# A two-layer hybrid encoder block on one core: start-up order, spread rope groups, a later transpose of the retention's output, and one early up chunk

## The chip, the core and the metric

The kernel runs on one core of a Trainium2 chip. Its engines work side by side, each from its own queue in its own order: TensorE (PE; the load of its stationary operand is listed as PEld), VectorE (DVE), ScalarE (ACT), GpSimd (POOL) and SyncE (SP, which issues most DMAs). An instruction waits for semaphores that other engines or DMAs raise, and everything behind it on its own queue waits with it. The metric is the device time in microseconds of one execution, in the median of the runs shown.

## What is computed

The reference runs two layers over a stream h of 512 tokens by 1024 channels in float32. Cut to what matters here:

```
u = rms_norm(h, norm_mix_pre[i])
proj = u @ w_in[i]
qa, ka, va, qr, kr, vr, gr, gate_a, gate_b = jnp.split(proj, splits, axis=-1)
att = dilated_attention_mixer(qa, ka, va)
ret = retention_mixer(qr, kr, vr, gr, ret_decay_logit[i])
merged = (jax.nn.sigmoid(gate_a) * (att @ w_att_out[i])
          + jax.nn.sigmoid(gate_b) * (ret @ w_ret_out[i]))
h = h + rms_norm(merged @ w_out[i], norm_mix_post[i])
u = rms_norm(h, norm_mlp_pre[i])
ff = jnp.square(jax.nn.relu(u @ w_mlp_up[i])) @ w_mlp_down[i]
h = h + rms_norm(ff, norm_mlp_post[i])
gate = jax.nn.sigmoid(rms_norm(h) @ w_ple_gate[i])
h = h + gate * rms_norm(p[i] @ w_ple_proj[i], norm_ple[i])
```

Attention has 8 heads of 64 channels, with rotary on 16 of them. Retention has 8 heads with keys of 64 and values of 128 channels, rotary on all key channels, two directions with a decay each, and each head's output is normalised over its 128 channels (group norm) before it is gated by silu(g).

## The kernel before

**Precision and weights.** Every float32 factor of a large product is split into a high part (an ACT copy to fp32r) and a low part (a subtraction, on DVE or POOL); each product is three matmuls, high by high, high by low and low by high (the table HL). The weights are packed on the host into chunks of 128 x 1024, in the order of the table PLAN. `prefetch` (L273) loads chunks on SP into tiles raw, copies the high part on ACT (L278) and subtracts the low part in `low` (L301); five split chunks (wt) are alive at a time, and `chunk` keeps about four ahead of their use. The low part of the kinds in POOL_LOW goes to POOL in two of three chunks, in two halves of 512 columns, and so do the chunks of POOL_MORE; all others go to DVE.

**Tokens.** The 512 tokens stand in four tiles of 128. `pre_norm` (L393) takes the sum of squares of a tile's two halves on ACT, adds 1e-6 to the first sum on DVE (L353), adds the two and takes the power -0.5 on POOL (`rstd_of`, L359 and L361), and scales on DVE (L403 or L406). Its inner function `rest` is put in a list: eight transposes on PE (L413), and the split into uT, high on ACT (L416), low on DVE (L417). `step` is called after each main step of PE, some six matmuls of 512 columns, and runs the oldest entry of the list when it is old enough. START gives these ages for tokens 1 to 3 at the start of the first layer.

**Order on PE.** PE's order is that of the program text (manual schedule); the other engines' order is made by the scheduler, by priority and readiness. The main jobs of a layer run in the order va, the attention's rope groups (q and k, twice), then rope q and k of the retention, vr, g 0 to 3, rope q and k, vr, and the a and g jobs. Beside them runs a generator `sides` (the attention's heads, then the retention's), which `tick` advances by 0.94 pieces for each main step from the end of the attention's rope groups on. A rope group is two chunks (8 main steps), and ends with some eight DVE and two ACT instructions of 512 columns.

**A retention head** (L583 to L633) is seven pieces: four score tiles (two matmuls each, L590 and L591, then a DVE product with the decay and a split into rt), `finish` of the head before (transposes of y, L576, and the gate), the product with v (12 matmuls, L612) with its ACT copy yt (L615), and the transposes of yt (L620) with the statistics (L624 to L627), the root on POOL (L628) and the scaling into y on DVE (L630). So between a head's L620 and its L576 stand the four score tiles of the next head. Behind the last head two empty pieces stand ahead of `finish`. `decay` makes the next head's decay table.

**Decays.** `decays` (L425) makes the logarithms of the decays from 32 numbers, in 25 small DVE instructions and one on ACT. It is called behind the va job of the first layer; its input tile dk comes by a DMA that is issued in it (L429).

**The up projection.** Behind w_out come eight products of the PLE projection (pp, evacuated in turn by ACT and DVE, L794 and L796), and then the first EARLY = 3 up chunks in two token halves (L871), 256 columns each: all chunks for tokens 0 and 1, and then all for tokens 2 and 3. The other up chunks run over all 512 tokens at once.

**The start.** L980 to L1005: token 0's rows in two halves, chunks 0 to 3, tokens 1 to 3, with `pre_norm` of token 0, its `rest` at once (flush), and the first splits between them.

Of the kernel before, what the change touches and what calls it, by code (L numbers as in the profile page):

```python
# [9 lines left out]
F32 = mybir.dt.float32  # L10
F32R = mybir.dt.float32r
# [18 lines left out]
POOL_MORE = [("pp",0),("pp",1)]  # L30
# [18 lines left out]
START = (2, 5, 7)  # L49
AGE_PP = 8  # L50
EARLY = 3
# [11 lines left out]
def _slot(e):  # L63
# [136 lines left out]
def block(ctx: ExitStack, tc: tile.TileContext, x, pT, w, dl, gains, cs, lc, rel, eye, out):  # L200
# [192 lines left out]
    def pre_norm(h, t, gain, upd=None):  # L393
        un = blk("P", [P, D], name="un")
        sq = []
        for n, sl in enumerate(HALVES):
            if upd:
                upd(sl)
            sq.append(sumsq(h[:, sl], un[:, sl], None if n else 1e-6))
        r = rstd_of(*sq)  # L400
        for sl in HALVES:
            if gain is None:
                nc.vector.tensor_scalar(un[:, sl], h[:, sl], r, None, op0=ALU.mult)  # L403
            else:
                g = gain[sl.start // S] if isinstance(gain, list) else gain[:, sl]
                nc.vector.scalar_tensor_tensor(un[:, sl], h[:, sl], r, g, op0=ALU.mult, op1=ALU.mult)  # L406

        def rest():
            unready.discard(t)
            for q in range(2):  # L410
                ps = bank("tp")
                for k in range(4):
                    nc.tensor.transpose(ps[:, k * P:(k + 1) * P], un[:, (4 * q + k) * P:(4 * q + k + 1) * P], ident)  # L413
                p3 = ps.rearrange("p (k n) -> p k n", k=4)
                hi = uT[:, 0, 4 * q:4 * q + 4, t * P:(t + 1) * P]
                nc.scalar.activation(hi, p3, AF.Copy)  # L416
                nc.vector.tensor_tensor(uT[:, 1, 4 * q:4 * q + 4, t * P:(t + 1) * P], p3, hi.bitcast(F32), op=ALU.subtract)  # L417

        unready.add(t)
        pending.append((clock[0], rest))  # L420
# [138 lines left out]
    def ret_heads(i, relt, gT, retT):  # L559
# [22 lines left out]

        for h in range(8):  # L583
# [4 lines left out]
            for k in range(NT):  # L588
# [11 lines left out]
                yield 1  # L600
            if late:
                finish(*late)
# [3 lines left out]
            y = t2("y")  # L606
            y3 = y.rearrange("p (t e) -> p t e", t=NT)
# [7 lines left out]
            nc.scalar.activation(yt, o, AF.Copy)  # L615
            yield 1
            o = bank("tp")
            o3 = o.rearrange("p (t e) -> p t e", t=NT)
            for t in range(NT):
                nc.tensor.transpose(o3[:, t, :], yt[:, t * P:(t + 1) * P], ident)  # L620
            mv = sm.tile([P, NT, 2], F32, name="mv", tag="mv", bufs=3)
            for t in range(NT):
                st = sm.tile([P, 6], F32, name="st", tag="st", bufs=4)
                nc.vector.bn_stats(st, o3[:, t, :])  # L624
                nc.vector.bn_aggr(mv[:, t, :], st)
            ve, rs = col(NT, name="ve"), col(NT, name="rs")
            nc.vector.tensor_scalar(ve, mv[:, :, 1], 1e-5, 16.0, op0=ALU.add, op1=ALU.mult)  # L627
            nc.gpsimd.tensor_tensor(rs, ve, half, op=ALU.pow)  # L628
            for t in range(NT):
                nc.vector.tensor_scalar(y3[:, t, :], o3[:, t, :], mv[:, t, 0:1], rs[:, t:t + 1],  # L630
                                        op0=ALU.subtract, op1=ALU.mult)
            yield 1
            late = (h, y3)  # L633
# [5 lines left out]
    def one_layer(i, h):  # L639
# [12 lines left out]
        if i == 0:  # L652
            decays()
# [107 lines left out]
        def evac_wo(hf):  # L761
            @soon
            def f(t, ps):
                hs_ = HALVES[hf]
                ssq[t][hf] = sumsq(ps, t2("junk"), None if hf else 1e-6)
# [20 lines left out]
        for hf in range(2):  # L786
            hsl = slice(hf * S, (hf + 1) * S)
            ch = chunk(i, "pp", hf)
            for t in range(NT):
                ps = bank(PP_BANKS[4 * hf + t])  # L790
                for k in range(2):
                    row_mm(ps, ch, k, lambda a, k, t: phl[k][:, a, t * P:(t + 1) * P], k, t, k == 0, k == 1)
                if t % 2:
                    nc.scalar.activation(pn[t][:, hsl], ps, AF.Copy)  # L794
                else:
                    nc.vector.tensor_copy(pn[t][:, hsl], ps)  # L796
                step(AGE_PP)
# [131 lines left out]
        def evac_dn(hf):  # L929
            @soon  # L930
            def f(t, ps):
                a = acc[t][hf]
                nc.vector.tensor_tensor(a, ps, a, op=ALU.subtract if hf else ALU.add)
                ssq[t][hf] = sumsq(a, t2("junk"), None if hf else 1e-6)
# [51 lines left out]
    nc.vector.memset(ones[:, :P], 1.0)  # L986
    prefetch(2, 0)
    nc.sync.dma_start(h[1], x[P:2 * P, :])
    prefetch(4, 0)
    for t in (2, 3):  # L990
# [46 lines left out]
```

## Time and profile before

| | us |
|---|---|
| median of 3 runs | 1794.63 (1794.54 to 1794.65) |
| the profiled execution | 1794.64 |
| its span, first to last instruction | 1792.9 |
| PE busy | 1772.4 (8209 matmuls) |
| DVE busy | 1145.4 |
| ACT busy | 807.5 |
| POOL busy | 382.6 |

Times in the profile are microseconds from the span's start, those marked ns excepted. L12 is line 12 of the kernel. A group's row has the line, the engine, the operation, its result and operands by the program's names, and how often it ran. The ends of matmuls are modelled, since they are pipelined: the distance from one matmul's start to the next tells more than the duration shown.

### The profile page before, as it was taken

How to read it: one execution, taken by the hardware profiler on the slowest of the kernel's cores; microseconds unless marked ns; L12 is line 12 of the kernel's file. 1: busy time of each engine (PE TensorE's matmuls, PEld its weight loads, DVE VectorE, ACT ScalarE, POOL GpSimd, SP SyncE). 2: the span in 40 equal slices, each digit the busy share in tenths (PEclk: the TensorE clock that was granted, in tenths of full speed). 3: DMA queues.
4: the chain of work that ended last, by engine and by line, in shares of the span. 5: the costliest groups of instructions: out<-in, count | busy, mean ns of one | idle time of the engine just before them, and what ended most of it. 6: DMA issues, size and time to landing. Idle time of an engine off the chain costs nothing.

```text
span 1792.9 us, 22127 instructions
## 1 busy us (share of the span) xinstructions
PE 1772.4 (99%) x8209; PEld 1466.2 (82%) x8209; DVE 1145.4 (64%) x1803; ACT 807.5 (45%) x1271; POOL 382.6 (21%) x354
## 2 busy tenths in 40 slices
PE   8999999999999999999999999999999999999998
PEld 6888788888898888888788887888888888888887
DVE  6676777743465677674656767677444657667754
ACT  4255444332466454433443555444333664444342
POOL 2312244311142001002123222442012410000030
PEclk9999999999999999999999999999999999999999
DMA  5555464552347655552346545555422566664421
GB/s 213 194 193 159 149 212 137 166 175 95 117 142 188 165 158 161 156 184 70 129 141 214 165 145 172 184 159 187 136 101 99 165 170 156 169 175 130 165 71 60
DMA packets 87807, 274.58 MB, mean 153 GB/s; under 512 B 11921, under 2 KB 20497, under 8 KB 87698
## 3 DMA queue, kind: packets, MB, share of 16 engines
q1 hardware_dynamic: 80786, 247.99, 40.7%
q0 software_dynamic: 6912, 25.17, 8.3%
q8 instruction: 65, 1.06, 0.2%
q14 instruction: 44, 0.36, 0.1%
HBM read 239.55 MB, written 33.55 MB: 152 GB/s over the span
## 4 chain that ended last, share of the span: by engine, by line
PE 89%; DVE 4%; POOL 2%; ACT 2%; issue 1%; DMA 1%; SPq 0%; POOLq 0%; ACTq 0%
PE acc L312 28%; PE acc L322 19%; PE s L312 18%; PE acc L849 8%; PE tp L849 4%; PE tp L612 2%; PE tp L544 2%; PE tp L507 2%; PE acc L871 1%; PE tp L413 1%; POOL wt L301 1%; PE s L525 1%; PE s L526 1%; PE s L590 1%; PE s L871 1%
## 5 line engine op out<-in xcount | busy, mean ns | idle before, releaser
L312 PE MATMUL acc<-uT,wt 128*128 128x512 f32 x1920 | 472.8, 392 | 0.0
L312 PEld LDWEIGHTS acc<-uT,wt 128*128 128x128 f32 x1920 | 356.2, 188 | 71.8
L301 DVE TENSOR_TENSOR wt<-raw,wt 128x1024 fp32r<-128x1024 f32 x217 | 279.4, 1292 | 187.6 <-ACT wt L278 187.1
L278 ACT ACTIVATE wt<-raw 128x1024 fp32r<-128x1024 f32 x280 | 293.9, 1055 | 223.0 <-PE acc L312 114.0
L322 PE MATMUL acc<-wt,uT 128*128 128x512 f32 x1320 | 320.8, 396 | 4.4 <-ACT uT L416 1.8
L312 PE MATMUL s<-uT,wt 128*128 128x512 f32 x1392 | 323.7, 389 | 0.0
L312 PEld LDWEIGHTS s<-uT,wt 128*128 128x128 f32 x1392 | 261.1, 188 | 54.1
L322 PEld LDWEIGHTS acc<-wt,uT 128*128 128x128 f32 x1320 | 245.6, 189 | 55.6 <-DVE uT L417 2.6
L301 POOL TENSOR_TENSOR wt<-raw,wt 128x512 fp32r<-128x512 f32 x126 | 173.2, 1395 | 408.1 <-ACT wt L278 339.1
L849 PE MATMUL acc<-wt,op 128*128 128x512 f32 x672 | 159.5, 389 | 0.0
L849 PEld LDWEIGHTS acc<-wt,op 128*128 128x128 f32 x672 | 126.1, 188 | 26.2
L268 POOL DMA_DIRECT2D wsum<-in_w_dram x48 | 42.8, 900 | 420.1 <-DVE wt L301 141.0
L892 ACT ACTIVATE relu<-s 128x512 f32<-128x512 f32 x60 | 35.7, 595 | 180.7 <-PE s L312 172.0
L860 DVE TENSOR_TENSOR sumP<-acc,sumP 128x512 f32<-128x512 f32 x92 | 61.8, 686 | 56.4 <-PE acc L849 56.1
L312 PE MATMUL acc<-retT,wt 128*128 128x512 f32 x384 | 89.3, 389 | 0.0
L322 PE MATMUL acc<-wt,ff 128*128 128x512 f32 x384 | 88.5, 390 | 0.0
L301 DVE TENSOR_TENSOR wt<-wsum,wt 128x1024 fp32r<-128x1024 f32 x48 | 60.6, 1263 | 41.7 <-ACT wt L278 41.7
L312 PEld LDWEIGHTS acc<-retT,wt 128*128 128x128 f32 x384 | 72.1, 188 | 15.0
L322 PEld LDWEIGHTS acc<-wt,ff 128*128 128x128 f32 x384 | 71.8, 188 | 14.8
L304 ACT ACTIVATE rt<-rz 128x512 fp32r<-128x512 f32 x64 | 40.3, 631 | 91.5 <-DVE rz L594 91.0
L849 PE MATMUL tp<-wt,op 128*128 128x512 f32 x336 | 80.7, 389 | 0.0
L849 PEld LDWEIGHTS tp<-wt,op 128*128 128x128 f32 x336 | 63.1, 188 | 13.1
(165 smaller groups left out, 2153.5 us busy)
## 6 DMA issues: line engine op xcount, KB each, us to landing
raw<-in_w_dram SPq DMA_DIRECT2D x280, 512.0 KB, 3.7
wsum<-in_w_dram POOLq DMA_DIRECT2D x48, 512.0 KB, 5.5
kk<-stk SPq DMA_DIRECT2D x128, 128.0 KB, 3.8
wsum<-in_w_dram SPq DMA_DIRECT2D x24, 512.0 KB, 3.3
stq<-rr SPq DMA_DIRECT2D x16, 512.0 KB, 3.4
qs<-stq SPq DMA_DIRECT2D x128, 64.0 KB, 2.9
stk<-rr SPq DMA_DIRECT2D x16, 512.0 KB, 3.0
stv<-vr SPq DMA_DIRECT2D x16, 512.0 KB, 4.4
```

Of the source, the lines that this page charges most:

```text
L268: nc.gpsimd.dma_start(r, rows(src[1]), accum_op=ALU.add)
L278: nc.scalar.activation(t[:, 0, :], r, AF.Copy)
L301: eng.tensor_tensor(dst, src, hi.bitcast(F32), op=ALU.subtract)
L304: nc.scalar.activation(dst[:, 0], src, AF.Copy, scale=scale)
L312: nc.tensor.matmul(ps, lhsT=t[:, a, (off + k) * P:(off + k + 1) * P], rhs=r, start=k == 0 and n == 0, stop=k == kts - 1 and n == 2)
L322: nc.tensor.matmul(ps, lhsT=lhs(a, k, t), rhs=ch[:, b, j * S:(j + 1) * S], start=first and n == 0, stop=last and n == 2)
L507: nc.tensor.matmul(o, lhsT=v, rhs=pt[k][:, hl, :], start=k == 0 and hl == 0, stop=k == 3 and hl == 1)
L544: nc.tensor.transpose(ps[:, t * P:(t + 1) * P], zs[t][:, k * P:(k + 1) * P], ident)
L612: nc.tensor.matmul(o, lhsT=v[:, k, a * P:(a + 1) * P], rhs=rt[k][:, b, :], start=n == 0, stop=n == 11)
L849: nc.tensor.matmul(ps, lhsT=op[:, a, k, j * P:(j + 1) * P], rhs=t[:, b, k * S:(k + 1) * S], start=k == 0 and n == 0, stop=k == 1 and n == 2)
L860: nc.vector.tensor_tensor(a, ps, a, op=ALU.add)
L871: nc.tensor.matmul(early[c][:, 256 * j:256 * j + 256], lhsT=t[:, a, k * P:(k + 1) * P], rhs=uT[:, b, k, 256 * j:256 * j + 256], start=k == ...
```

## The change

It has these parts. At the start the order of ACT and DVE is written by hand, chunk 0 is loaded and split in two halves, each ahead of one half of token 0's transposes, and token 1's norm is cut in two around the split of chunk 2; token 1's transposes come one step later. The tile dk is loaded at the start, and `decays` is called behind the attention's rope groups. The four first g jobs stand between the retention's rope groups, and vr 0 behind the third of them. The 1e-6 is added on POOL with the second sum. A retention head's transposes of yt and its statistics (now `normed`) move behind the second score tile of the next head. EARLY is 1. The low parts of the pp chunks go to DVE, and all pp products are evacuated on ACT.

```
-POOL_MORE = [("pp",0),("pp",1)]
+POOL_MORE = []
-START = (2, 5, 7)
+START = (3, 5, 7)
-EARLY = 3
+EARLY = 1
...
-    + [("qr", c) for c in range(2)] + [("kr", c) for c in range(2)]
-    + [("vr", c) for c in range(4)]
-    + [("g", c) for c in range(4)]
-    + [("qr", 2 + c) for c in range(2)] + [("kr", 2 + c) for c in range(2)]
-    + [("vr", 4 + c) for c in range(4)]
+    + [("g", 0), ("g", 1), ("qr", 0), ("qr", 1), ("g", 2), ("kr", 0), ("kr", 1), ("g", 3), ("qr", 2), ("qr", 3)]
+    + [("vr", c) for c in range(4)] + [("kr", 2), ("kr", 3)] + [("vr", 4 + c) for c in range(4)]
...
-            nc.gpsimd.tensor_tensor(r, a, b, op=ALU.add)
+            nc.gpsimd.tensor_scalar(r, a, b, 1e-6, op0=ALU.add, op1=ALU.add)
...
+        def quarter(q):
+            ps = bank("tp")
+            for k in range(4):
+                nc.tensor.transpose(ps[:, k * P:(k + 1) * P], un[:, (4 * q + k) * P:(4 * q + k + 1) * P], ident)
...
+        def in_steps():
+            r = root()
+            yield
+            scaled(r)
+            queue()
...
+    dk = tmp.tile([P, S], F32, name="dk", tag="g", bufs=4)
+
     def decays():
-        dk = t2("dk")
-        nc.sync.dma_start(a, dl.to_broadcast([P, n]))
...
                 if k == 0 and h < 7:
                     qk, vh = load_qk(i, 1, h + 1), load_v(i, h + 1)
                 yield 1
+                if k == 1 and late:
+                    late = normed(*late)
+                    yield 1
             if late:
                 finish(*late)
             yield 1
...
             yt = t2("yt")
             nc.scalar.activation(yt, o, AF.Copy)
+            late = (h, yt)
             yield 1
...
-            yield 1
-            late = (h, y3)
+        yield 1
+        late = normed(*late)
         yield 1
         yield 1
         finish(*late)
...
-        if i == 0:
-            decays()
...
         side["gen"], side["rate"], side["owed"] = sides(), RATE, 0.0
+        if i == 0:
+            decays()
         cr = cs_tile(1)
+        g_job(0)
+        g_job(1)
         rope_group(i, 1, 0, cr, "q")
+        g_job(2)
         rope_group(i, 1, 0, cr, "k")
+        g_job(3)
+        rope_group(i, 1, 1, cr, "q")
         vr_job(0)
-        for c in range(4):
-            g_job(c)
-        rope_group(i, 1, 1, cr, "q")
         rope_group(i, 1, 1, cr, "k")
         vr_job(1)
...
-                if t % 2:
-                    nc.scalar.activation(pn[t][:, hsl], ps, AF.Copy)
-                else:
-                    nc.vector.tensor_copy(pn[t][:, hsl], ps)
+                soon(nc.scalar.activation)(pn[t][:, hsl], ps, AF.Copy)
...
+    raw[0] = blk("A", [P, D], name="raw")
+    for sl in HALVES:
+        nc.sync.dma_start(raw[0][:, sl], rows(0)[:, sl])
+    loaded[0] = 1
     prefetch(2, 0)
     nc.sync.dma_start(h[1], x[P:2 * P, :])
     prefetch(4, 0)
+    nc.sync.dma_start(dk[:, :NL * 16], dl.to_broadcast([P, NL * 16]))
...
-    pre_norm(h[0], 0, g0)
-    prefetch(4, 1)
-    flush()
-    prefetch(4, 2)
-    pre_norm(h[1], 1, g0)
-    prefetch(4, 4)
+    with tc.manual_schedule(engines={mybir.EngineType.Activation, mybir.EngineType.DVE}):
+        pre_norm(h[0], 0, g0)
+        parts = pending.pop(0)[1](parts=True)
+        wt[0] = wp.tile([P, 2, 1024], F32R, name="wt", tag="wt", bufs=5)
+        for sl in HALVES:
+            nc.scalar.activation(wt[0][:, 0, sl], raw[0][:, sl], AF.Copy)
+            low(nc.vector, wt[0][:, 1, sl], raw[0][:, sl], wt[0][:, 0, sl])
+            next(parts, None)
+        next(parts, None)
+        raw.pop(0)
+        loaded[1] = 1
+        prefetch(4, 2)
+        r1 = pre_norm(h[1], 1, g0, steps=True)
+        next(r1)
+        prefetch(4, 3)
+        next(r1, None)
+        prefetch(4, 4)
```

In `normed` stand the lines of before, from the transposes of yt to the scaling into y.

## Rows read from the trace of the kernel before

**Rows 1.** The page, part 1: busy us (share of the span) and instructions.
```profile
PE 1772.4 (99%) x8209; PEld 1466.2 (82%) x8209; DVE 1145.4 (64%) x1803; ACT 807.5 (45%) x1271; POOL 382.6 (21%) x354
```

**Rows 2.** The chain that ended last, in order of time: start, us, what.
```profile
521.51 5.76 PE acc L871 x48
...
552.26 5.44 PE s L312 x24
```

**Rows 3.** Waits of PE, whole run: us in total, times, longest.
```profile
PE tp L544 <- DVE pt L301: 3.5, 2, 1.7
PE tp L413 <- DVE uT L417: 2.9, 2, 1.5
PE tp L620 <- ACT yt L615: 2.0, 5, 0.6
```

**Rows 4.** Timeline of PE, first 46 us: start, us, what, [idle before <-releaser].
```profile
10.76 1.22 PE L322 MATMUL acc<-wt,uT 128*128 128x512 f32 x2 [1.80 <-ACT uT L416]
12.14 4.58 PE L322 MATMUL acc<-wt,uT 128*128 128x512 f32 x10 [0.15 <-DVE uT L417]
...
20.30 2.79 PE L322 MATMUL acc<-wt,uT 128*128 128x512 f32 x11 [1.09 <-DVE ss L353]
...
32.21 9.40 PE L322 MATMUL acc<-wt,uT 128*128 128x512 f32 x40 [1.32 <-DVE uT L417]
```

**Rows 5.** Timeline of all engines, first 60 us.
```profile
6.11 1.41 DVE L406 SCALAR_TENSOR_TENSOR un<-h,rstd,acc 128x512 f32<-128x512 f32 x2 [1.43 <-POOL rstd L361]
...
7.89 1.06 ACT L278 ACTIVATE wt<-raw 128x1024 fp32r<-128x1024 f32 x1 [2.72 <-DMA raw<-in_w_dram]
...
19.03 1.22 DVE L301 TENSOR_TENSOR wt<-raw,wt 128x1024 fp32r<-128x1024 f32 x1
...
26.66 0.43 SPq L429 DMA_DIRECT2D dk<-in_dl_dram  x1
...
31.38 0.18 DVE L430 TENSOR_SCALAR dk<-dk 128x32 f32<-128x32 f32 x1 [4.40 <-DMA dk<-in_dl_dram]
```

**Rows 6.** Timeline of all engines, 484 to 546 us.
```profile
520.38 1.28 DVE L417 TENSOR_TENSOR uT<-tp,uT 128x512 fp32r<-128x512 f32 x2
```

**Rows 7.** Timeline of the retention's heads 0 and 1, first layer.
```profile
254.51 0.60 PE L620 MATMUL tp<-ident,yt 128*128 128x128 f32 x4
...
259.66 1.04 DVE L630 TENSOR_SCALAR y<-tp,mv,rs 128x128 f32<-128x128 f32 x3
...
268.21 1.52 PE L312 MATMUL acc<-uT,wt 128*128 128x512 f32 x6
...
270.20 0.66 PE L620 MATMUL tp<-ident,yt 128*128 128x128 f32 x4 [0.47 <-ACT yt L615]
...
276.37 1.04 DVE L630 TENSOR_SCALAR y<-tp,mv,rs 128x128 f32<-128x128 f32 x3
```

**Rows 8.** Timelines of PE, POOL and DVE, last head of the first layer.
```profile
365.69 0.60 PE L620 MATMUL tp<-ident,yt 128*128 128x128 f32 x4
...
370.23 0.60 PE L576 MATMUL tp<-ident,y 128*128 128x128 f32 x4
...
367.86 1.04 POOL L628 TENSOR_TENSOR rs<-ve,neghalf 128x4 f32<-128x4 f32 x1 [0.42 <-DVE ve L627]
...
368.93 1.36 DVE L630 TENSOR_SCALAR y<-tp,mv,rs 128x128 f32<-128x128 f32 x4 [1.17 <-POOL rs L628]
```

**Rows 9.** Groups of DVE by form: busy us, mean ns | idle before, releaser.
```profile
L301 DVE TENSOR_TENSOR rt<-rz,rt 128x512 fp32r<-128x512 f32 x48 | 46.3, 972 | 9.8 <-ACT rt L304 9.0
...
L627 DVE TENSOR_SCALAR ve<-mv 128x4 f32<-128x4 f32 x16 | 4.7, 294 | 0.6
```

**Rows 10.** Timeline of all engines, 834 to 870 us.
```profile
862.56 1.04 POOL L359 TENSOR_TENSOR rstd<-ss 128x1 f32<-128x1 f32 x1 [2.79 <-ACT uT L416]
...
865.79 1.26 PE L413 MATMUL tp<-ident,un 128*128 128x128 f32 x8 [1.47 <-DVE uT L417]
```

**Rows 11.** Timeline of all engines, 190 to 216 us.
```profile
213.06 0.66 PE L544 MATMUL tp<-ident,z 128*128 128x128 f32 x4 [1.71 <-DVE pt L301]
```

More of the change, by code (lines that the diff above doesn't have):

```diff
@@ L391, in settle, with pre_norm, root, scaled @@
             soon(pending.pop(0)[1])()
-    def pre_norm(h, t, gain, upd=None):
+    def pre_norm(h, t, gain, upd=None, steps=False):
         un = blk("P", [P, D], name="un")
[L395 to L403, printed above, removed]
-            else:
-                g = gain[sl.start // S] if isinstance(gain, list) else gain[:, sl]
-                nc.vector.scalar_tensor_tensor(un[:, sl], h[:, sl], r, g, op0=ALU.mult, op1=ALU.mult)
-        def rest():
+        def root():
+            sq = []
+            for sl in HALVES:
+                if upd:
+                    upd(sl)
+                sq.append(sumsq(h[:, sl], un[:, sl]))
+            return rstd_of(*sq)
+        def scaled(r):
+            for sl in HALVES:
+                if gain is None:
+                    nc.vector.tensor_scalar(un[:, sl], h[:, sl], r, None, op0=ALU.mult)
+                else:
+                    g = gain[sl.start // S] if isinstance(gain, list) else gain[:, sl]
+                    nc.vector.scalar_tensor_tensor(un[:, sl], h[:, sl], r, g, op0=ALU.mult, op1=ALU.mult)
+        def quarter(q):
+            ps = bank("tp")
+            for k in range(4):
+                nc.tensor.transpose(ps[:, k * P:(k + 1) * P], un[:, (4 * q + k) * P:(4 * q + k + 1) * P], ident)
+            p3 = ps.rearrange("p (k n) -> p k n", k=4)
+            hi = uT[:, 0, 4 * q:4 * q + 4, t * P:(t + 1) * P]
+            nc.scalar.activation(hi, p3, AF.Copy)
+            nc.vector.tensor_tensor(uT[:, 1, 4 * q:4 * q + 4, t * P:(t + 1) * P], p3, hi.bitcast(F32), op=ALU.subtract)
+        def rest(parts=False):
@@ L409, in rest @@
             unready.discard(t)
+            if parts:
+                return (quarter(q) for q in range(2))
             for q in range(2):
[L411 to L416, printed above, removed]
@@ L417, in rest, with queue @@
-                nc.vector.tensor_tensor(uT[:, 1, 4 * q:4 * q + 4, t * P:(t + 1) * P], p3, hi.bitcast(F32), op=ALU.subtract)
-        unready.add(t)
-        pending.append((clock[0], rest))
+                quarter(q)
+        def queue():
+            unready.add(t)
+            pending.append((clock[0], rest))
+        def in_steps():
[3 more added lines that the diff above has]
+            queue()
+        if steps:
+            return in_steps()
+        scaled(root())
@@ L422, in block @@
+        queue()
     lg = cst.tile([P, NL * 16], F32, name="lg")
     nlg = cst.tile([P, NL * 16], F32, name="nlg")
+    dk = tmp.tile([P, S], F32, name="dk", tag="g", bufs=4)
     def decays():
         n = NL * 16
-        dk = t2("dk")
         a, e, z, q, acc = (dk[:, j * n:(j + 1) * n] for j in range(5))
-        nc.sync.dma_start(a, dl.to_broadcast([P, n]))
         nc.vector.tensor_scalar(e, a, -1.0, None, op0=ALU.mult)
@@ L581, in finish, with normed @@
             retT.append(b)
+        def normed(h, yt):
+            y = t2("y")
+            y3 = y.rearrange("p (t e) -> p t e", t=NT)
+            o = bank("tp")
+            o3 = o.rearrange("p (t e) -> p t e", t=NT)
+            for t in range(NT):
+                nc.tensor.transpose(o3[:, t, :], yt[:, t * P:(t + 1) * P], ident)
+            mv = sm.tile([P, NT, 2], F32, name="mv", tag="mv", bufs=3)
+            for t in range(NT):
+                st = sm.tile([P, 6], F32, name="st", tag="st", bufs=4)
+                nc.vector.bn_stats(st, o3[:, t, :])
+                nc.vector.bn_aggr(mv[:, t, :], st)
+            ve, rs = col(NT, name="ve"), col(NT, name="rs")
+            nc.vector.tensor_scalar(ve, mv[:, :, 1], 1e-5, 16.0, op0=ALU.add, op1=ALU.mult)
+            nc.gpsimd.tensor_tensor(rs, ve, half, op=ALU.pow)
+            for t in range(NT):
+                nc.vector.tensor_scalar(y3[:, t, :], o3[:, t, :], mv[:, t, 0:1], rs[:, t:t + 1],
+                                        op0=ALU.subtract, op1=ALU.mult)
+            return h, y3
         for h in range(8):
@@ L615, in ret_heads @@
             nc.scalar.activation(yt, o, AF.Copy)
+            late = (h, yt)
             yield 1
[L617 to L631, printed above, removed]
-            yield 1
-            late = (h, y3)
+        yield 1
+        late = normed(*late)
         yield 1
@@ L764, in f @@
                 hs_ = HALVES[hf]
-                ssq[t][hf] = sumsq(ps, t2("junk"), None if hf else 1e-6)
+                ssq[t][hf] = sumsq(ps, t2("junk"))
                 nc.vector.tensor_tensor(acc[t][:, hs_], ps, g_post[:, hs_], op=ALU.mult)
@@ L986, in block @@
     nc.vector.memset(ones[:, :P], 1.0)
+    raw[0] = blk("A", [P, D], name="raw")
+    for sl in HALVES:
+        nc.sync.dma_start(raw[0][:, sl], rows(0)[:, sl])
+    loaded[0] = 1
     prefetch(2, 0)
@@ L995, in block @@
     warm_up(WARM2)
-    pre_norm(h[0], 0, g0)
-    prefetch(4, 1)
-    flush()
-    prefetch(4, 2)
-    pre_norm(h[1], 1, g0)
-    prefetch(4, 4)
+    with tc.manual_schedule(engines={mybir.EngineType.Activation, mybir.EngineType.DVE}):
+        pre_norm(h[0], 0, g0)
+        parts = pending.pop(0)[1](parts=True)
+        wt[0] = wp.tile([P, 2, 1024], F32R, name="wt", tag="wt", bufs=5)
+        for sl in HALVES:
+            nc.scalar.activation(wt[0][:, 0, sl], raw[0][:, sl], AF.Copy)
[10 more added lines that the diff above has]
+        prefetch(4, 4)
     for t in (2, 3):
```

5 lines of the change are left out of this document (1 added, 4 removed).

## The prediction

> **What bounds the kernel now.** I read the page's first part, then the waits of TensorE (PE), then the timeline of each place that they name. PE is busy for 1772.4 us of a span of 1792.9 [rows 1], and in the body the matmuls stand at their own rate: 24 of 512 columns take 5.44 us, 0.227 us each [rows 2]. So time can only go in two ways: PE gets less work, or one of its few waits goes. These are small and in known places: transposes of the attention (L544) behind VectorE (DVE), transposes of the pre-norm (L413) behind the low part of uT, and the retention's L620 behind the ACT copy yt, 2.0 us in five waits [rows 3]. Besides these there is the start, where PE works at about half rate and with gaps until 20.30 us, and stops once more before 32.21 us [rows 4]. All that can be won is some 20 us. The profiled run took 1794.64 us, 1.74 us around the span; the median of the runs is 1794.63, so the sum is made against 1794.64. About 0.2% (3.6 us) is what a measurement of this kernel can tell from no change.
>
> **The start.** Before, the first matmul of the first layer runs at 10.76 us. Ten matmuls at 12.14 take 4.58 us, 0.43 each, which is the rate of the lower clock level of 1.2 GHz; at 20.30 the 20th matmul begins, after a wait [rows 4], for the low part of the fourth weight chunk, on DVE from 19.03 to 20.25 [rows 5]. The change sets ACT's and DVE's order by hand and splits chunk 0 and token 0 by halves. The scaled halves of token 0 are there from 6.1 to 7.5 us as before; the first half's four transposes and its ACT copy no longer queue behind the whole-chunk copies of 7.89 us [rows 5], so the first matmul can start near 8.4. From there PE needs 18 matmuls at 0.43 (7.7 us) and eight transposes (1.0) before chunk 3: 17.1 us. DVE has, from 7.5 us, four low parts of 1.22 [rows 5], token 0's two halves of uT (1.28, the duration in [rows 6]) and token 1's scaling (1.41): 7.6 us, so 15.1 if it never waits for ACT, and I allow 2 us for the hand-overs: 17.1 too. The 20th matmul then stands at 17.3 in place of 20.30: -3.0 us. Bounds: if the first half of chunk 0 lands no sooner than the whole did (7.89), everything is about 1.1 later; if DVE waits at every hand-over, the gain is 0; if the clock rises earlier because the work starts earlier, -4.
>
> Then the decays. Their tiny DMA is issued behind weight loads, and its first DVE instruction (31.38 us, after 4.40 us of waiting) holds up the uT subtraction queued behind it; PE waits 1.32 us for that at 32.21 [rows 4, 5]. The change loads dk at the start and moves the 25 small DVE instructions behind the attention's rope groups, where g jobs (one DVE instruction each) follow instead of rope: -1.3 (bounds -1.5 and 0). On SP's queue two issues of 0.43 us [rows 5] come earlier (chunk 0 has two, dk stands ahead of tokens 2 and 3); token 1's rows are wanted only after chunk 1's copy, so I cost them at nothing; if they were late, the list on ACT would wait 0.4 us for each. Token 2's transposes come where DVE is still catching up: +0.2 (0 to +1). Sum of the start **-4.1**.
>
> **One early up chunk.** 48 matmuls of 256 columns take 5.76 us, the same chunk whole 5.44 [rows 2]. Two chunks in each of two layers go back to whole: 4 x 0.32 = **-1.3**. What the cover was for: the second token half now begins at about 521.3, not 527.1, and its second matmul needs the low part of uT of tokens 2 and 3, which DVE writes from 520.38 to 521.66 [rows 6], the first four of eight slices by 521.0. It fits by a few tenths, and the PLE copies that leave DVE (all on ACT now) make room in front of it; against this stand two weight low parts of 1.22 [rows 5] that come from POOL to DVE in each layer, both ahead of token 3's work. 0, bounds 0 and +2.
>
> **Retention.** Removed: the wait for yt. In head 1 six matmuls issued at 268.21 are through at 269.57 by their rate, and L620 starts at 270.20 [rows 7]: 0.63 lost where the view shows 0.47, since ends are modelled. So the five waits' 2.0 us [rows 3] are about **-2.7**. Now yt has two score steps to be ready.
>
> What is late next is y. Between the transposes of yt and `finish` stood five main steps (six matmuls, 1.36 us each) and four score pairs; now three steps and two pairs remain. In the last head, with nothing between, transposes at 365.69 and finish at 370.23 stand 4.54 apart, three steps and 0.46 for the transposes themselves [rows 8]. So in the new order finish comes 0.46 + 3 x 1.36 + 2 x 0.45 = 5.4 us after the transposes, and its last transpose at 5.8. The chain (statistics on DVE, the root on POOL, four scalings on DVE) takes 4.60 us at its best: POOL at +2.17, the scalings from +3.24 to +4.60 [rows 8]. Undisturbed heads fit. But in head 0 the last scaling ends at 260.70, +6.2, and in head 1 at 277.41, +7.2 [rows 7]; of the 14 heads that have a head behind them these are a middling and the worst one. The new window has as many score products, and two low parts of rt on DVE in place of one on POOL. I take half of the 14 heads 0.5 late: **+3.5** (bounds 0 and +14).
>
> The last head of each layer loses one step: the generator passes an empty step, then normalises, one empty step, then finish. So finish stands at 0.46 + 2 x 1.36 = 3.2 after the transposes, its last part at 3.5, and the chain at its best ends at 4.6: 1.1 in each layer, **+2.2** (bounds +2 and +4). I know of nothing that hides it.
>
> DVE and POOL disturb each other here: the scaling `ve`, four elements wide, takes 0.29 in the mean of 16 heads, and the low parts of rt 0.97 in the mean [rows 9], where a low part of uT of the same size takes 0.64 [rows 6]. The Trainium skill ("SBUF — State Buffer", Who interferes with whom) says that a DVE instruction with two SBUF inputs and a POOL instruction that reads SBUF exclude each other for a whole instruction, whichever comes first. The means agree with that, and it speaks against this edit, which puts more two-input work beside POOL's root; by the rows the term is +3.5, and with one blocked instruction in every head, as the rule allows, it would be near its upper bound.
>
> **The rest.** The 1e-6 goes from a DVE instruction into POOL's add. At 862.56 that add starts only when DVE has finished a weight's low part, and PE waits 1.47 at 865.79 for the uT low part behind it [rows 10]; two such places: -0.3 each, **-0.6** (bounds 0 and -3; POOL's two-scalar form is not in the trace, and costs at least the add's time). Rope spread: the costliest wait, 1.71 us at 213.06 [rows 11], comes with the rope group that ends on the 64th main step behind the attention's start, beside the transposes of head 6. In the new order the second k group still ends on the 64th step, so I expect this wait to stay in both layers, and only small ones to go: **-0.4** (bounds -4 and +3).
>
> Sum: -4.1 - 1.3 - 2.7 + 3.5 + 2.2 - 0.6 - 0.4 = -3.4, so 1791.2 us.
>
> **Rivals.**
> Finish never waits in the 14 heads, because the scheduler puts y first on DVE: -3.4 - 3.5 = -6.9, 1787.7 us. For it: 4.60 against 5.8 at its best. Against it: 6.2 and 7.2.
> The start gains only the wait for dk, because chunk 0's halves land late or DVE and ACT wait for each other in the fixed order: -3.4 + 2.8 = -0.6, 1794.0 us. For it: the DMA queue is full there, and everything hangs on one list.
> Slower: y is late in all 14 heads, since POOL's root and DVE's low parts queue behind one another. Without the finish term the sum is -6.9, so at 0.49 us a head nothing is left, and from 0.75 it is slower by over 0.2%; at 1.0, between the middling head (6.2 against 5.8) and the worst (7.2), +14: 1801.7 us. It is here that the skill's rule on the shared port would decide.
> That the spread does not do what it says (the wait at the 64th step returns) is part of my forecast; were it wrong, it would add up to -3.8.
>
> **How the numbers follow.** Forecast 0.45, finish free 0.25, start without gain 0.15, slower 0.15. The forecast's own range, 1789 to 1793.5, lies about half on each side of 1791.0. So faster 0.21 + 0.25 = 0.46, same 0.24 + 0.15 = 0.39, slower 0.15. The range takes in the finish-free case with a little of the start's upper bound, the case without gain, and the milder part of the slower one: 1786.5 to 1797.
>
> **What would show it.** Right: the first matmul near 8.4, the 20th near 17.3, and no gap before the last 40 of the row job; L620's line without waits; L576's line, which had none, with waits for y, 1.1 us in the last head of each layer and some tenths in about half of the others; 96 matmuls of 256 columns in the early chunks in place of 288; the wait of L544 near the 64th step still there. Wrong: waits of the second token half for uT, many waits of L576 over 0.75, or a wait of the attention's first transposes behind the decays, which would put the time above the range.

## The result, and the profile after

The changed kernel takes 1813.29 us (1811.12 to 1816.32 in 4 runs) against 1794.59 for the kernel before in the same comparison: a ratio of 1.0105 [1.0092, 1.0118], 18.7 us slower. 1791.2 had been forecast, and the range ended at 1797.0. The profiled execution is the longest of the four, 1816.32 us with a span of 1814.6.

The page's first part, after the change (its line before: [rows 1]):

```profile
PE 1783.9 (98%) x8113; PEld 1467.8 (81%) x8113; DVE 1132.1 (62%) x1760; ACT 813.7 (45%) x1280; POOL 376.3 (21%) x346
```

96 matmuls are gone, as meant, and yet PE is busy for 11.5 us longer while the span has grown by 21.7. So there are two losses: PE waits more, and some of its matmuls run longer. The waits of PE (us in total, times, longest), for [rows 3]:

```profile
PE tp L594 <- DVE y L617: 16.5, 18, 1.7
PE tp L562 <- DVE z L550: 3.3, 4, 0.9
PE tp L412 <- DVE uT L416: 1.7, 2, 0.9
PE tp L412 <- DVE un L404: 1.6, 4, 0.6
...
PE s L543 <- DVE nm L547: 0.9, 2, 0.5
```

The three lines of [rows 3] have gone or shrunk. In their place stands one that was not there at all: the transposes of y in `finish` (L594, before L576) wait for the scaling on DVE. The view's 16.5 us count too little, since ends of matmuls are modelled. From the start of the matmul ahead of a head's four transposes to the start of the one behind them, the 16 heads take 33.8 us together where they took 9.4. That is **24.4 us**, 4.5 of it in the two last heads and 19.9 in the fourteen others.

Head 0 of the first layer on all engines, for the first lines of [rows 7]:

```profile
255.77 0.60 PE L607 MATMUL tp<-ident,yt 128*128 128x128 f32 x4
...
258.72 0.17 DVE L614 TENSOR_SCALAR ve<-mv 128x4 f32<-128x4 f32 x1
258.97 1.03 POOL L615 TENSOR_TENSOR rs<-ve,neghalf 128x4 f32<-128x4 f32 x1 [2.51 <-DVE ve L614]
...
260.04 0.41 DVE L617 TENSOR_SCALAR y<-tp,mv,rs 128x128 f32<-128x128 f32 x1 [1.15 <-POOL rs L615]
...
260.37 0.68 DVE L632 TENSOR_TENSOR rz<-s,T 128x512 f32<-128x512 f32 x1
260.96 0.40 DVE L617 TENSOR_SCALAR y<-tp,mv,rs 128x128 f32<-128x128 f32 x1
...
261.25 0.50 PE L594 MATMUL tp<-ident,y 128*128 128x128 f32 x2
261.28 0.68 DVE L632 TENSOR_TENSOR rz<-s,T 128x512 f32<-128x512 f32 x1
...
261.88 1.16 DVE L298 TENSOR_TENSOR rt<-rz,rt 128x512 fp32r<-128x512 f32 x1
...
262.96 0.72 DVE L617 TENSOR_SCALAR y<-tp,mv,rs 128x128 f32<-128x128 f32 x2
...
263.42 0.65 PE L594 MATMUL tp<-ident,y 128*128 128x128 f32 x2 [1.67 <-DVE y L617]
```

The root is ready at +4.2 us behind the transposes of yt, and four scalings that followed one another would end at +5.6, in time for `finish` at +5.5 to +5.8. But DVE's queue puts two score products (rz) and a low part of rt between them, and the last scaling ends at 263.68, +7.9. The same holds in every one of the 14 heads: the last scaling ends at +6.1 to +8.0, 7.3 in the mean.

The second loss is TensorE's clock. Windows of PE after the change (us, then busy time and instructions of PE, PEld, DVE, ACT, POOL, then the granted clock, DMA share and GB/s):

```profile
94.70:98.10 3.40, 3.40 (x12) 2.74 (x12) 0.69 (x2) 1.20 (x2) 0.00 (x0) 0.51 0.85 219
299.50:302.90 3.40, 3.40 (x9) 2.63 (x9) 2.47 (x4) 2.67 (x4) 0.98 (x1) 0.51 1.04 343
381.40:384.80 3.40, 3.40 (x9) 2.62 (x9) 1.63 (x4) 1.89 (x3) 0.00 (x0) 0.51 1.00 393
1163.10:1166.50 3.40, 3.40 (x9) 2.61 (x8) 2.25 (x3) 2.53 (x3) 0.34 (x1) 0.52 0.89 287
1279.10:1282.50 3.40, 3.40 (x10) 2.64 (x9) 1.75 (x3) 1.84 (x3) 0.00 (x0) 0.51 0.95 366
```

Five times in this execution the clock falls from 2.4 to 1.2 GHz for 3.4 us, each time just behind waits of PE (0.9 to 1.7 us; two of 0.6 and 0.7 in the second case). In the profiled execution of the kernel before it stayed at 2.4 GHz in the whole body. The timeline of PE at two of these places, the first with a row from before the fall:

```profile
89.25 2.89 PE L309 MATMUL acc<-uT,wt 128*128 128x512 f32 x12
...
94.44 0.36 PE L562 MATMUL tp<-ident,z 128*128 128x128 f32 x1 [0.86 <-DVE z L550]
94.53 2.84 PE L309 MATMUL acc<-uT,wt 128*128 128x512 f32 x6
...
379.39 1.28 PE L594 MATMUL tp<-ident,y 128*128 128x128 f32 x4 [1.41 <-DVE y L617]
380.43 4.59 PE L309 MATMUL acc<-attT,wt 128*128 128x512 f32 x12
```

Twelve matmuls that take 2.89 us at the upper level (at 89.25) take 4.59 behind 380.43. One fall costs 3.4 us at half rate, 1.7 us; five make **8.5**. The four runs bear this out: those with a mean clock of 0.995 and 0.996 took 1816.32 and 1815.13, those with 0.998 took 1811.45 and 1811.12.

The account of the profiled executions: +24.4 (y) + 8.5 (clock) = 32.9, and 21.7 was measured, so the rest gains 11.2 us. Of these, 3.2 are the waits for yt, which are gone (the transposes of yt take 9.4 us from start to start, counted in the same way, where they took 12.6). The experiments tell what the other 8.0 are.

### The profile page after: what moved, and what is told of

Its sections match the earlier page's. It is cut to its first block, busy times and chain, and to the rows that moved or that the text cites. A ratio compares the mean times of both kernels' runs of the same rounds, so it can differ in the third digit from the quotient of the medians.

```text
span 1814.6 us, 21912 instructions
## 1 busy us (share of the span) xinstructions
PE 1783.9 (98%) x8113; PEld 1467.8 (81%) x8113; DVE 1132.1 (62%) x1760; ACT 813.7 (45%) x1280; POOL 376.3 (21%) x346
## 4 chain that ended last, share of the span: by engine, by line
PE 75%; DVE 5%; POOL 2%; ACT 2%; issue 1%; POOLq 0%; ACTq 0%; DVEq 0%
PE acc L309 20%; PE s L309 19%; PE acc L319 16%; PE acc L873 8%; PE tp L873 4%; PE tp L651 2%; PE tp L412 1%; DVE rz L632 1%; PE tp L525 1%; DVE rt L298 1%; PE tp L562 1%; POOL rs L615 1%; ACT rt L301 1%; PE s L895 1%; DVE y L617 1%
## 5 line engine op out<-in xcount | busy, mean ns | idle before, releaser
L298 DVE TENSOR_TENSOR wt<-raw,wt 128x1024 fp32r<-128x1024 f32 (+1 forms) x222 | 287.0, 1298 | 183.0 <-ACT wt L275 182.3
L309 PE MATMUL s<-uT,wt 128*128 128x512 f32 x1488 | 345.4, 389 | 0.0
L309 PEld LDWEIGHTS s<-uT,wt 128*128 128x128 f32 x1488 | 279.2, 188 | 57.9
L298 POOL TENSOR_TENSOR wt<-raw,wt 128x512 fp32r<-128x512 f32 x118 | 158.0, 1359 | 369.8 <-ACT wt L275 312.3
```

Source lines behind the costliest of these rows:

```text
L298: eng.tensor_tensor(dst, src, hi.bitcast(F32), op=ALU.subtract)
L309: nc.tensor.matmul(ps, lhsT=t[:, a, (off + k) * P:(off + k + 1) * P], rhs=r, start=k == 0 and n == 0, stop=k == kts - 1 and n == 2)
```

## The experiments

The theory was that the retention edit alone makes the loss, because y comes late behind other work on DVE, and that the clock adds to it; the rivals, that a part of the start or of the rope order does harm, or that the wait lies in the chain itself (statistics, root, scaling) and not in the order. No run leaves a part of the computation out.

**Retention as before, the rest changed**

```
-        def normed(h, yt):
...
-                if k == 1 and late:
-                    late = normed(*late)
-                    yield 1
...
+            o = bank("tp")
+            o3 = o.rearrange("p (t e) -> p t e", t=NT)
...
+            late = (h, y3)
```

> The changed kernel with the retention head as before (transposes of yt one step behind their product) and every other part of the change kept. Theory (the time is lost where finish waits for y, and in the lower clock that follows the longest of these waits): both go, about 18 us of waits and four of the five low-clock stretches of 3.4 us, 1.7 us each; the yt waits return with some 2 us; from 1813 to 1816 down to 1789 to 1793 us. Rival (the loss is in the other parts, the start, the spread or the single early chunk, and only shows at finish): over 1805 us.

1788.27 us, 0.9969 [0.9958, 0.998]: the other parts together gain 5.7 (6.2 by the spans of the profiled executions, 1786.7 against 1792.9). The account above leaves them 8.0; the 1.8 between the two stays open. The same kernel ran once more beside later ones:

> The changed kernel with the retention head as before, once more on this chip, as a look beside the others: 1788 to 1789.5, with the five waits for yt, 2.0 us in the view. Against the kernels with the transposes behind the first score tile it shows what the edit of the retention is worth when y is in time: 1 to 3 us in their favour.

1789.33 us in one execution (a span of 1787.6 against 1786.7 for the first profile). The second one had a clock fall behind the waits at 94 us and the first, with waits of the same length there, had none; at 1.7 a fall is more than the 0.9 between their spans.

**The retention edit alone**, on the kernel before (the diff above the other way round):

```
+        def normed(h, yt):
...
+                if k == 1 and late:
+                    late = normed(*late)
+                    yield 1
```

> The kernel before with the retention part of the change alone. Theory: slower by about as much as the changed kernel and a little more, since the gains of the other parts are missing: 1811 to 1820 us, with waits of finish of 16 to 19 us in sum. Rival (other parts): within 3 us of 1794.6.

1819.80 us, 1.0144 [1.0129, 1.0159]. PE's waits in it:

```profile
PE tp L576 <- DVE y L599: 16.6, 18, 1.7
```

The same 18 waits of the same size. The edit alone costs 25.8 us and the rest gains 5.7, and 25.8 - 5.7 = 20.1 stands near the 18.7 measured for both. So the loss is the retention edit's.

**One score step earlier**

```
-                if k == 1 and late:
+                if k == 0 and late:
...
-        yield 1
         late = normed(*late)
         yield 1
         yield 1
+        yield 1
```

> The changed kernel with the transposes of yt behind the first score tile of the next head in place of the second, and in the last head right behind the product. Finish then has one main step and one score pair more, 1.81 us. In the changed kernel y ends 6.1 to 8.0 us after the transposes; finish needs it at 5.8, then at 7.6. Theory: waits of finish under 2 us in sum, no low-clock stretch behind them, 1786 to 1791 us. Rival (y is late because its work is queued behind whatever scores follow, however much room there is): waits stay at over 8 us, over 1800 us.

1786.95 us, 0.996 [0.9946, 0.9975]. No wait for y is left. The transposes of head 0 on PE:

```profile
254.33 0.60 PE L607 MATMUL tp<-ident,yt 128*128 128x128 f32 x4
...
261.62 0.60 PE L594 MATMUL tp<-ident,y 128*128 128x128 f32 x4
```

7.3 us lie between them, where the change leaves 5.5. This one step is worth 26.3 us against the changed kernel, and yt still has a step to be ready in. Its one run at a clock of 1.0 took 1785.55, against about 1788.1 for the runs at 1.0 with the retention of before: by that single run the waits for yt were worth some 2.5 (3.2 from start to start in the traces). The chain itself is no shorter here: the last scaling ends at +6.0 to +7.8, 7.1 in the mean of the 14 heads. It is in time since PE comes later.

**The same place, ahead on DVE**

```
-                    late = normed(*late)
+                    late = soon(normed)(*late)
...
-        late = normed(*late)
+        late = soon(normed)(*late)
```

> The changed kernel with the transposes where it has them, but the scheduler told to put the statistics, the root and the scalings first on DVE and POOL. If the order on DVE makes y late (in the changed kernel the four scalings are cut apart by score products and low parts), y ends near 5 to 5.8 and the waits of finish fall from 16.5 us to 3 to 6 (the two last heads keep theirs, 1.5 each): 1790 to 1797 us. If the length of the chain itself does (POOL's root, hand-overs), waits stay over 10 us and the time over 1803 us.

1791.57 us, 0.9987 [0.9977, 0.9997]. PE's wait for y, and DVE in head 0:

```profile
PE tp L594 <- DVE y L617: 3.2, 3, 1.4
```

```profile
258.42 1.37 DVE L617 TENSOR_SCALAR y<-tp,mv,rs 128x128 f32<-128x128 f32 x4 [1.14 <-POOL rs L615]
259.70 1.28 DVE L632 TENSOR_TENSOR rz<-s,T 128x512 f32<-128x512 f32 x2
```

Nothing but priority differs, the four scalings stand together in all heads, and the waits of L594 shrink to three. Two of these are the last heads, where a weight's low part of 1.2 us still stands among the statistics on DVE. The last scaling of the other 14 ends at +5.5 in the mean in place of +7.3. So it is the order on DVE that makes 14 heads late, and not the length of the chain.

**Dummy matmuls in the waits**

```
+FILL = (8, 0, 14, 0)
...
             for t in range(NT):
+                for _ in range(FILL[t]):
+                    nc.tensor.matmul(ps[:, t * P:(t + 1) * P], lhsT=warm, rhs=warm, start=True, stop=True)
                 nc.tensor.transpose(ps[:, t * P:(t + 1) * P], y3[:, t, :], ident)
```

> The changed kernel with 22 small bf16 matmuls put into each finish (8 ahead of its first transpose, 14 ahead of its third), whose results are overwritten; they leave out nothing and run while PE would wait for y. The waits themselves stay, since y comes when it comes. If the low-clock stretches come from PE standing still in these waits: they go or get rarer, and the time falls by what they cost, 1.7 us each, to 1807 to 1811 us. If they have nothing to do with it: as many as in the changed kernel, 1811 to 1818 us.

1812.77 us (1812.41 to 1813.23), 1.0101 [1.0087, 1.0115]. 352 small matmuls were added. A window of the last head, where the changed kernel's clock fell:

```profile
380.00:384.00 4.00, 4.00 (x19) 3.31 (x18) 3.33 (x6) 3.41 (x5) 0.00 (x0) 1.00 1.01 406
```

The clock stayed at 2.4 GHz (1.0 in all four runs), and the times, which ranged over 5.2 us, range over 0.8. So the falls behind the waits for y hang on PE standing still, and they make the scatter of these runs. The fall at the attention's first transposes, where no dummies were put, is missing too; it comes in some executions only, so four without it prove little. The time lies some 2 us above what was expected: I had not reckoned with what the dummies cost in heads where y is hardly late. The 16 finishes take 38.7 us from start to start where they took 33.8, and these 4.9 take back most of the 6.8 of four falls. The median is no better than the change's, so nothing is won by this.

**The start alone**, on the kernel before (the decays at their old place in the text, dk loaded early, the 1e-6 on POOL; cut):

```
-START = (2, 5, 7)
+START = (3, 5, 7)
...
-            nc.gpsimd.tensor_tensor(r, a, b, op=ALU.add)
+            nc.gpsimd.tensor_scalar(r, a, b, 1e-6, op0=ALU.add, op1=ALU.add)
...
+    nc.sync.dma_start(dk[:, :NL * 16], dl.to_broadcast([P, NL * 16]))
...
+    with tc.manual_schedule(engines={mybir.EngineType.Activation, mybir.EngineType.DVE}):
+        pre_norm(h[0], 0, g0)
+        parts = pending.pop(0)[1](parts=True)
```

> The kernel before with the start's part of the change alone: order of ACT and DVE by hand, chunk 0 in halves, dk loaded at the start, the 1e-6 on POOL; the decays stay behind the va job. By the prediction's term: 4.1 us less, 1790 to 1791, the first matmul of a chunk near 8.4 to 9.3, no wait near 31 us. If the start's gain only moves a wait elsewhere: within 1 us of before.

1796.84 us, 1.0013 [1.0004, 1.0022]: 2.0 more than the kernel before, so the gain is not to be seen in the time. The timeline shows it at the start (first chunk matmul at 8.82 in place of 10.76) and lost 500 us later, in each layer:

```profile
511.62 0.68 DVE L817 COPY pn<-acc 128x512 f32<-128x512 f32 x1
...
512.22 0.68 DVE L817 COPY pn<-s 128x512 f32<-128x512 f32 x1
...
512.35 1.84 PE L322 MATMUL acc<-wt,phl 128*128 128x512 f32 x6 [2.12 <-DVE pn L817]
```

A product of the PLE projection waits for its bank, which a copy on DVE empties late: 4.2 us in two waits, and a clock fall behind the first. The kernel before has the same copies and no such wait; why they come late here was not tried.

**The same with the PLE copies on ACT**

```
-                if t % 2:
-                    nc.scalar.activation(pn[t][:, hsl], ps, AF.Copy)
-                else:
-                    nc.vector.tensor_copy(pn[t][:, hsl], ps)
+                soon(nc.scalar.activation)(pn[t][:, hsl], ps, AF.Copy)
```

> The start's part alone once more, with all pp products evacuated on ACT as in the change. In the run without this a new wait stands in each layer, 2.1 us for a DVE copy of pn, and behind one of them a low-clock stretch. If that took the start's gain: both waits go, 4.2 us and up to 1.7 less than that run, 1790 to 1791.5. If the start itself gains nothing: 1795 to 1797 again.

1792.94 us, 0.9991 [0.9982, 1.0]. These waits are gone, and 3.9 us with them, but of a start that ends 4.35 earlier only 1.6 reach the time, and the time lies 1.4 above what I expected. The waits of PE:

```profile
PE tp L415 <- DVE uT L419: 3.0, 4, 0.8
```

Two of these four, 0.69 in the timeline at 512.66 and its like in the second layer, are new and stand beside the PLE products. From start to start they cost 1.7 of the missing 2.8. By the spans of the profiled executions (1790.3 against 1792.9) 2.6 of the 4.35 come through, and these two waits are nearly all that is missing; the 1.0 between spans and medians stays open.

**The rope order alone**

```
+    + [("g", 0), ("g", 1), ("qr", 0), ("qr", 1), ("g", 2), ("kr", 0), ("kr", 1), ("g", 3), ("qr", 2), ("qr", 3)]
...
+        g_job(0)
+        g_job(1)
         rope_group(i, 1, 0, cr, "q")
+        g_job(2)
         rope_group(i, 1, 0, cr, "k")
...
+        g_job(3)
         rope_group(i, 1, 1, cr, "q")
+        vr_job(0)
```

> The kernel before with the order of the g jobs and rope groups of the change alone. By the prediction's term: about 0.4 less, the wait of L544 near the 64th step (1.7 in each layer) still there. By the changed kernel's trace, where this wait is gone and one of 0.6 to 0.7 stands in each layer at a score tile instead: 2 to 3 us less, 1791 to 1793.

1791.61 us, 0.9982 [0.9973, 0.9991], -3.2 (2.2 by the spans of the profiled executions). Where PE waited 1.71 us in [rows 11], its timeline now has no wait, and a smaller one stands elsewhere in the waits of PE:

```profile
212.13 0.60 PE L541 MATMUL tp<-ident,z 128*128 128x128 f32 x4
212.49 3.02 PE L319 MATMUL acc<-wt,uT 128*128 128x512 f32 x12
```

```profile
PE s L522 <- DVE nm L526: 0.9, 2, 0.5
```

**One early up chunk alone**

```
-EARLY = 3
+EARLY = 1
```

> The kernel before with one up chunk in two token halves in place of three, nothing else. By the term: 1.3 us less (4 chunks, 5.76 to 5.44 us each), no new wait of the second half; 1792.5 to 1793.5. If the cover was needed: a wait of L871 for uT and no gain, or a loss up to 2 us.

1793.24 us, 0.9991 [0.9982, 0.9999], -1.6, and no new wait of the second token half. The chain's rows for [rows 2], in the changed kernel (one chunk in halves, and a later one whole):

```profile
530.08 5.74 PE s L895 x48
...
563.05 5.44 PE s L309 x24
```

**One step earlier, and the decays called where they were**

```
-                if k == 1 and late:
+                if k == 0 and late:
...
         row_job([(i, "va", c) for c in range(4)], u_lhs, evac_va, VA_GRP[i], AGE_VA)
+        if i == 0:
+            decays()
...
-        if i == 0:
-            decays()
         cr = cs_tile(1)
```

> The changed kernel with the transposes of yt behind the first score tile, and the decays behind the va job of the first layer as in the kernel before (dk still loaded at the start). If the decays' DVE instructions make the wait of the first attention transposes near 92 us in the first layer (2.1 us, now and then with a low-clock stretch): it falls to the 0.4 of before, 2 us less than with the transposes moved alone, 1783.5 to 1786. If it comes from the order of the g jobs (in the second layer, which has no decays, 1.9 us stand there): no difference, 1786 to 1788.

1783.10 us (1783.03 to 1783.68), 0.9939 [0.9925, 0.9953], 0.4 below what was expected: it beats both kernels, and the one without the move of the decays by 3.85 (in another comparison; by the spans of the profiled executions, 1785.4 and 1781.9, by 3.5). In the changed kernel the attention's first transposes wait twice near 93 us. DVE and POOL there, first in the changed kernel, then DVE and PE in this one:

```profile
90.30 2.61 POOL L298 TENSOR_TENSOR wt<-raw,wt 128x512 fp32r<-128x512 f32 x2 [4.74 <-ACT wt L275]
...
91.69 1.51 DVE L550 TENSOR_SCALAR z<-z,rd 128x512 f32<-128x512 f32 x1
93.12 0.68 DVE L710 SCALAR_TENSOR_TENSOR gT<-th,acc 128x512 f32<-128x512 f32 x1
...
93.90 0.49 DVE L550 TENSOR_SCALAR z<-z,rd 128x512 f32<-128x512 f32 x1
```

```profile
89.52 0.69 DVE L712 SCALAR_TENSOR_TENSOR gT<-th,acc 128x512 f32<-128x512 f32 x1 [0.21 <-ACT th L710]
...
92.10 0.49 DVE L550 TENSOR_SCALAR z<-z,rd 128x512 f32<-128x512 f32 x1
92.32 0.65 PE L562 MATMUL tp<-ident,z 128*128 128x128 f32 x4
```

With the decays in the old place gT stands ahead of the last two scalings of z and not between them, and PE waits for neither: that is 2.1 us from start to start (1.8 against the kernel before, where 0.4 was lost there), and the clock fall of 1.7 behind it, which not every execution has. The order of the g jobs is not the cause: in the run with the rope order alone, whose decays are at the old place, PE has no wait here either. Two things make z late, and no run separates them: gT, of 0.68, and the scaling at 91.69 itself, which takes 1.51 us where most take 0.49 and ends 0.29 behind POOL's low part (in this kernel its like takes 1.09, and ends 0.29 behind POOL's too). It is not the decays' instructions that are in the way: since dk is there early, they run at 23.5 to 33.2 us in the changed kernel and at 23.9 to 33.6 in this one. So it is their place in the text, by the order that the scheduler gives DVE later, that makes the wait. Why the order changes with it was not tried.

**Both remedies together**

```
-                if k == 1 and late:
-                    late = normed(*late)
+                if k == 0 and late:
+                    late = soon(normed)(*late)
...
+        if i == 0:
+            decays()
```

> The same, with the statistics, the root and the scalings also first on DVE and POOL. With the room of one score step more y was in time without it, so no more than 0.5 either way from the run without priority; if priority holds up score products (PE waits at the score tiles), slower by 1 to 3.

1787.13 us, 0.9962 [0.9949, 0.9974], 4.0 more than without priority, and 1.0 more than the worst that was expected. Now the score products are late:

```profile
PE s L628 <- DVE rz L632: 2.8, 4, 1.4
```

So where there is room, priority wins nothing and holds up the score products. Alone it did not do that: the run with priority and no room has no such wait, and it won 21.7 of the 26.3 us that room won.

## Why the prediction was wrong

**The step that failed** is "I take half of the 14 heads 0.5 late: +3.5". All 14 are late, and their finishes take 1.4 longer in the mean, which makes 19.9, more than the bound of 14. I had the right window (5.4 to 5.8, measured 5.5 in twelve heads and 6.8 in two) and the right row: in [rows 7] the scalings of heads 0 and 1 ended at +6.2 and +7.2, and both are past it. I called them "a middling and the worst one" and let half of the heads off, since the chain at its best ends at 4.60. That best is the last head [rows 8], where no score products queue on DVE. The row nearest to the 14 heads was the +6.2: in the trace of before 11 of the 14 end past +5.8, and their mean is 6.1. By that row all of them are late by 0.4 to 0.8, which makes 6 to 11 us and still not 19.9.

The other part of the step's error is that I took the chain at the length that it had in its old place ("The new window has as many score products"). It grew with the move: the last scaling ends at +7.3 in the mean, 1.2 later, and nearly all of that lies between the first scaling and the last, which stand 3.1 us apart from start to end in place of 2.0. The scheduler puts more score products and low parts of rt between them there, and the run with priority, where all four take 1.37, shows that this is what makes them late.

For a larger size I had only DVE and POOL disturbing each other. The Trainium skill ("SBUF — State Buffer", Who interferes with whom) has them shut each other out of their shared port, and by it the term would have stood near its upper bound. No run shows that the port decides here: the scaling `ve` takes 0.26 us in the mean after the change and the low parts of rt 0.87, not more than the 0.29 and 0.97 of [rows 9], and the run with priority, which has the same instructions, loses most of the waits. Single instructions are held even so (the low part of rt at 261.88 takes 1.16 where most take 0.69); how much of the 14 heads' lateness hangs on such ones no run separates.

**What was missing** from the sum is the clock. No term said that PE, when it has stood still for a microsecond, may then run at half rate for 3.4 us: 8.5 us in the profiled execution, four of five falls behind the retention's new waits. The rows before could not show it, because in that execution it did not happen in the body, though a wait of 1.71 [rows 11] was there.

**The last heads**, +2.2 forecast: the two finishes take 4.5 more from start to start, past the bound of 4. It was right in kind, and half the size. I took the chain at its best, 4.60; in its new place it ends at +5.7, since a weight's low part of 1.19 us (at 376.27) stands among the statistics on DVE. The run with one step more has no wait there.

**The start**, -4.1: right in its sum, in part by luck. Its timeline on PE, for [rows 4]:

```profile
9.29 4.96 PE L319 MATMUL acc<-wt,uT 128*128 128x512 f32 x13
14.67 1.43 PE L319 MATMUL acc<-wt,uT 128*128 128x512 f32 x5 [0.43 <-DVE wt L298]
...
16.73 2.28 PE L319 MATMUL acc<-wt,uT 128*128 128x512 f32 x8
...
24.75 12.51 PE L319 MATMUL acc<-wt,uT 128*128 128x512 f32 x54
```

The first matmul comes at 9.29 (forecast 8.4), the 20th, second in the row at 16.73, near 17.0 (forecast 17.3), and the row job ends at 24.75 + 12.51 = 37.26 in place of 32.21 + 9.40 = 41.61: -4.35. The first matmul was 0.9 late, and the 18 ahead of chunk 3 then took 6.65 us (9.29 to 15.94) in place of the 7.7 I gave them, since from about 12.9 us on they stand 0.23 apart and not 0.43: two errors that cancel. I had read the 0.43 as the lower clock level. It is the distance that matmuls have in the five falls too, but the granted clock reads 1.00 at the start (10.76 to 16.50 before, 9.29 to 16.70 after), so no row shows that level there. A sign that I had named as wrong did come, the wait of the attention's first transposes, and with its clock fall it takes back 3.5. I had costed the move of the decays by their 25 instructions; these are harmless, and their place in the order is not.

**The early chunk**, -1.3: measured -1.6. **The waits for yt**, -2.7: 3.2 from start to start. **The 1e-6 on POOL**, -0.6: no gain to be seen. The wait of [rows 10] shrank to 0.81, at 876.55 in the changed kernel, and its like in the second layer with it:

```profile
876.55 1.25 PE L412 MATMUL tp<-ident,un 128*128 128x128 f32 x8 [0.81 <-DVE uT L416]
```

But waits of the same transposes for un grew, from 0.7 to 1.6 us, and from start to start the transposes of the pre-norm lose 4.9 us behind the start in both kernels. The add itself takes 0.30 us at the least in its new form, and 0.19 in the old one. Whether the 1e-6 makes any of this was not tried by itself.

**The rope order**, -0.4: wrong in its reason. "In the new order the second k group still ends on the 64th step, so I expect this wait to stay": the wait went, and the term is -3.2, inside the bounds. I had tied the wait to where the group ends; that it hangs on how much of the groups' work still stands on DVE then is my reading, and no run shows it.

Put together: -4.35 + 3.5 - 1.6 - 3.2 (yt) - 3.2 (rope order) + 19.9 + 4.5 + 6.8 (four falls) = +22.35, against +21.7 of span; 0.65 is left over. The two terms from runs, -1.6 and -3.2, are differences of medians, whose intervals reach 1.5 us to either side.

Of the rivals the slower one had late heads in all 14, at 1.0 each where 1.4 was measured. It was given 15%, and its cause, POOL's root and DVE's low parts behind one another, was not the one that the runs showed.

## What to carry to other kernels

When a step is moved to gain room on one side, measure the room on the other side against the **typical** end of its chain in the busy places of the trace, not against its best, and expect the chain to change length in its new place. On an engine that works in order, a chain is as long as what the scheduler puts between its links: here four scalings of 0.34 us took 3.6. A call of a small piece of work is a place in that order too, even where its instructions run long before. Of the two remedies alone, room (one step more) beat priority by 4.6 us, most of it in the two last heads, and priority on top of room cost 4.0.

## What was not expected of the hardware

TensorE's granted clock fell from 2.4 to 1.2 GHz for 3.4 us behind waits of 0.6 to 1.7 us between dense matmuls, with 1.7 us lost each time. Not each such wait does it. Two of the same length in one execution are the wait that ends at 263.42, shown above, and this one:

```profile
1161.45 0.65 PE L594 MATMUL tp<-ident,y 128*128 128x128 f32 x2 [1.67 <-DVE y L617]
```

Behind this one the clock fell at 1163.0 (the window from 1163.10 is shown above). Behind the one at 263.42 it stayed:

```profile
263.40:268.00 4.60, 4.58 (x20) 3.69 (x21) 3.92 (x6) 2.48 (x3) 0.52 (x1) 1.00 1.00 307
```

What sets the one apart from the other stays open. With small matmuls in the waits there was no fall in any of four runs.
